# Rows of x and B through VectorE transposes and DRAM in a hybrid SSD / short-conv / gated decoder step

## The chip, the cores and the metric

The kernel runs on 1 core of one Trainium2 chip. The metric is the device time of one execution in microseconds. The profile is one more execution of the same program with the hardware profiler on. The engines are named as in the profile: PE is TensorE, DVE is VectorE, ACT is ScalarE, POOL is GpSimd, SP is SyncE, which issues most transfers.

## The reference, cut to what matters

One layer of a decoder step is computed in float32 for 336 tokens (16 meta tokens, 256 prompt tokens, 8 samples of 8 tokens) with D_MODEL 2048. The normalised tokens go through one input projection, whose columns feed two branches. Branch A is a state-space scan (SSD) over 64 heads of 64 columns, in 8 groups of 8 heads; each group shares one B and one C of 128 states. Branch B is a short gated convolution. Both are gated, merged and projected once more.

```python
xbc = silu(causal_dwconv(xbc, conv_prev, ssd_conv_w) + ssd_conv_b)
xs, bm, cm = split(xbc)                        # x: 64 heads x 64, B and C: 8 groups x 128
dt = softplus(dt_raw + dt_bias); log_a = dt * -exp(a_log); acum = cumsum(log_a)
wts = (cm . bm) * exp(acum_i - acum_j) * dt_j  # within a chunk, causal
y_diag = wts @ xs
chunk_states = sum_j exp(acum_last - acum_j) * dt_j * xs_j * bm_j
h = exp(acum_last) * h + chunk_states          # carried over the chunks; h0 for the samples
y = y_diag + (cm . h_in) * exp(acum) + d_skip * xs
y = group_rms_norm(y * silu(z)) * ssd_norm_w;  y_a = y @ w_ssd_out
x + (sigmoid(g_a) * y_a + sigmoid(g_b) * y_b) @ w_o
```

The outputs are the tokens after a final RMS norm and the new convolution and scan states.

## The kernel before, in words

**Layout.** Channels lie on partitions and tokens on the free axis, so a projection's 128 output channels come out as a tile of 128 x 320 to 336. A weight block is 128 x 1024 numbers (512 KB). `wblk` (L90) loads it on SP into `wraw`, ACT copies it into the rounded half `whi` (L94) and DVE makes the rest `wlo` (L96); each of the three has three buffers. `mm` (L108) multiplies it with the two halves of the tokens: `whi` by the high and the low half (L111, L112), `wlo` by the high half (L115), 24 matmuls for a block. A unit of a projection is two blocks that gather in one PSUM tile `pj` (two buffers). PSUM further has `ms` (two buffers) and `yb` (four banks).

**Stages.** First come the norm, branch B and the gates that need no scan, with the decay tables in between. Then the scan stage goes over the 8 groups g. In it these units run, each with its matmuls: four `z_units(g)` (the gate z, L496), eight `out_units(g-1)` (the projection of the group before, L733; one block each), six `conv_units(g+1)` (the convolution of the next group's B, C and four tiles of x, L481), and in the first and the last group four `gate_units`. The output projection ends the program.

**The scan as steps.** `ssd(g)` (L514) is a generator that does the scan of group g in steps, one at each `yield`. `weave` (L775) spreads a group's 23 steps over the units of the same group in proportion to their weights: z first, then out, gate, conv. `behind` (L99) binds the instructions of a step to come after the last weight block's on ACT, DVE and PE; within that the order on each engine is set by the planner of the framework, which also orders SP's transfers.

**What the change touches.** The scan needs x and B with tokens on partitions. `rows(c)` (L530), called for the three chunks of tokens (128, 128 and 80), makes them on PE: four transposes of x (L534) and one of B (L536) against the identity into two `ms` tiles, and beside them the product of B and C (L537). DVE scales x by dt from PSUM (L539), ACT and DVE split B in two halves (L546, L547) or copy it (L542), and DVE masks the product (L551). Further steps: `decay` (L554), `weights` (L564), `halve` (L572, splits the scaled x into the one buffer `xw`), `state` (L582, the chunk's state on PE), then `po` (L636, the samples' old states) and `yb` (L650, the scan's output). After that the samples' rows are put in order through the DRAM buffers `xq_d` and `bq_d` (L669 to L687), the norm of the group is made (L692 to L705), the samples' new states are made and stored (L713 to L719), and `yh`, `yl` (L722 to L728) are what `out_units` multiplies in the group that follows. The old states `h0` are loaded by four transfers of 512 KB in one step (L605 to L609).

## Time and profile before

| what | value |
|---|---|
| time, median of 3 runs (lowest to highest) | 1823.0 us (1822.77 to 1824.39) |
| time of the profiled execution | 1824.75 us |
| its span, first to last instruction | 1823.0 us |
| PE busy | 1814.9 us |
| DVE, ACT, POOL busy | 1147.7, 828.8, 389.4 us |
| granted PE clock | 1.0 |
| one group of the scan stage (902.00 to 1013.45 us) | 111.45 us, DVE 84.94, ACT 60.45, POOL 42.72 us busy |
| DMA in that group | 0.63 of the 16 engines, 201 GB/s |

A row of the groups' view reads: line, engine, operation, tiles out<-in, shapes, count, then the busy time, the mean of one in ns, and the idle time of the engine just before with what ended it. A row of the timeline reads: start, duration, engine, line, operation and tiles, count, and in brackets the idle time before it with what ended it. PE's matmuls overlap: each is shown from its issue to its end, so the cost of one on PE is the distance from its start to the next one's start.

### The profile page before, as it was taken

Reading aid. Unit: us, or ns where it says so; the run is one execution under the profiler, and the core shown is the slowest. Engines: PE = TensorE matmul, PEld = TensorE weight load, DVE = VectorE, ACT = ScalarE, POOL = GpSimd, SP = SyncE. Lnnn points to the kernel's source line nnn. Section 1 sums busy time; section 2 is a strip of 40 time slices with the busy share of each in tenths; the row PEclk is TensorE's granted clock in tenths of the full one; section 3 lists DMA queues with packets and bytes.
Section 4 is the critical chain, followed back from the end, with each engine's and each line's share of the span. In section 5 each row is a group of like instructions: output and inputs, shape, how many; then the busy total and the mean of one; then the engine's idle time right before and its main releaser. Section 6 shows DMA issues by size and latency. Waiting matters only on the chain.

```text
span 1823.0 us, 32410 instructions
## 1 busy us (share of the span) xinstructions
PE 1814.9 (100%) x13006; PEld 1798.0 (99%) x13006; DVE 1147.7 (63%) x1696; ACT 828.8 (45%) x1269; POOL 389.4 (21%) x398
## 2 busy tenths in 40 slices
PE   9999999999999999999999999999999999999998
PEld 9999999999999999999999999999999999999998
DVE  7745544444543335668587787877778777776544
ACT  6433333333333334645656354564546545343543
POOL 0000000000000001253162433524334252400012
PEclk9999999999999999999999999999999999999999
DMA  7444444444444446457566574665656657476553
GB/s 254 146 151 150 150 149 149 145 152 151 156 152 159 160 162 227 149 178 240 163 201 223 177 246 150 208 215 178 238 157 211 206 169 249 153 243 213 184 175 129
DMA packets 117286, 331.33 MB, mean 182 GB/s; under 512 B 20944, under 2 KB 37904, under 8 KB 117136
## 3 DMA queue, kind: packets, MB, share of 16 engines
q1 hardware_dynamic: 116272, 327.89, 55.9%
q8 instruction: 102, 1.67, 0.4%
q10 hardware_dynamic: 864, 1.38, 0.2%
q14 instruction: 48, 0.39, 0.1%
HBM read 296.34 MB, written 32.88 MB: 181 GB/s over the span
## 4 chain that ended last, share of the span: by engine, by line
PE 96%; DMA 2%; ACT 1%; DVE 1%; issue 0%; POOLq 0%; POOL 0%; SPq 0%; ACTq 0%; DVEq 0%
PE pj L111 30%; PE pj L112 30%; PE pj L115 29%; PE yb L650 2%; DMA wraw<-w 1%; PE ms L636 1%; PE pj L219 1%; PE yb L585 1%; PE pj L862 1%; ACT whi L94 0%; PE ms L534 0%; ACT W L559 0%; PE ms L219 0%; DMA ssms<-h 0%; PE yb L713 0%
## 5 line engine op out<-in xcount | busy, mean ns | idle before, releaser
L111 PE MATMUL pj<-hx,whi 128*128 128x320 f32 (+3 forms) x2880 | 864.4, 312 | 0.0
L112 PE MATMUL pj<-hx,whi 128*128 128x320 f32 (+3 forms) x2880 | 860.6, 311 | 0.0
L96 DVE TENSOR_TENSOR wlo<-wraw,whi 128x1024 fp32r<-128x1024 f32 x470 | 596.8, 1270 | 413.9 <-ACT whi L94 206.8
L94 ACT ACTIVATE whi<-wraw 128x1024 fp32r<-128x1024 f32 x470 | 496.7, 1057 | 768.0 <-PE pj L112 628.1
L111 PEld LDWEIGHTS pj<-hx,whi 128*128 128x128 f32 x2880 | 540.7, 188 | 4.6 <-ACT pad L462 1.7
L112 PEld LDWEIGHTS pj<-hx,whi 128*128 128x128 f32 x2880 | 541.5, 188 | 0.1
L115 PE MATMUL pj<-hx,wlo 128*128 128x320 f32 (+3 forms) x2880 | 485.4, 310 | 0.0
L115 PEld LDWEIGHTS pj<-hx,wlo 128*128 128x128 f32 x2880 | 440.6, 188 | 0.0
L111 PE MATMUL pj<-yh,whi 128*128 128x320 f32 x512 | 153.5, 311 | 1.2 <-ACT zs L503 0.9
L112 PE MATMUL pj<-yl,whi 128*128 128x320 f32 x512 | 152.3, 309 | 0.0
L596 POOL TENSOR_TENSOR h<-h,decS 128x512 f32<-128x512 f32 x64 | 76.4, 1227 | 147.5 <-PE ms L636 147.5
L111 PEld LDWEIGHTS pj<-yh,whi 128*128 128x128 f32 x512 | 96.2, 188 | 3.1 <-ACT zs L503 1.4
L112 PEld LDWEIGHTS pj<-yl,whi 128*128 128x128 f32 x512 | 96.3, 188 | 0.6
L115 PE MATMUL pj<-yh,wlo 128*128 128x320 f32 x512 | 95.8, 309 | 0.0
L242 POOL COPY SCS<-up 128x2 f32<-128x2 f32 x16 | 18.2, 1139 | 359.2 <-DVE up L236 329.0
L744 DVE TENSOR_TENSOR yan<-yan,pj 128x320 f32<-128x320 f32 x112 | 54.2, 485 | 62.9 <-PE pj L115 61.3
L471 DVE SCALAR_TENSOR_TENSOR cacc<-pad,V,cacc 128x360 f32<-128x360 f32 (+1 forms) x144 | 89.5, 621 | 2.0
L464 POOL COPY pad<-cs 128x24 f32<-128x24 f32 x48 | 56.2, 1172 | 126.6 <-DVE cacc L471 115.5
L115 PEld LDWEIGHTS pj<-yh,wlo 128*128 128x128 f32 x512 | 80.4, 188 | 0.0
L111 PE MATMUL pj<-vhi,whi 128*128 128x320 f32 x256 | 75.5, 308 | 0.0
L112 PE MATMUL pj<-vlo,whi 128*128 128x320 f32 x256 | 75.5, 308 | 0.0
L465 POOL COPY cs<-pad 128x3 f32<-128x3 f32 x48 | 45.0, 938 | 82.5 <-ACT pad L462 82.0
(286 smaller groups left out, 1721.7 us busy)
## 6 DMA issues: line engine op xcount, KB each, us to landing
wraw<-w SPq DMA_DIRECT2D x346, 512.0 KB, 3.9
wraw<-wso SPq DMA_DIRECT2D x64, 512.0 KB, 3.5
wraw<-wsc SPq DMA_DIRECT2D x32, 512.0 KB, 3.8
h<-h0T SPq DMA_DIRECT2D x32, 512.0 KB, 4.9
ssms<-h SPq DMA_DIRECT2D x32, 512.0 KB, 4.2
wraw<-wo SPq DMA_DIRECT2D x32, 512.0 KB, 3.9
xq_d<-xe SPq DMA_DIRECT2D x16, 320.0 KB, 3.4
W<-ac_d SPq DMA_DIRECT2D x8, 576.0 KB, 6.4
```

What stands on the lines that cost most here:

```text
L94: latest["act"] = nc.scalar.activation(hi[:, :n], raw[:, :n], AF.Copy).ins
L96: latest["dve"] = nc.vector.tensor_tensor(lo[:, :n], raw[:, :n], fb(hi[:, :n]), sub).ins
L111: nc.tensor.matmul(out, w, xh(k0 + k), start=first and k == 0, stop=False)
L112: nc.tensor.matmul(out, w, xl(k0 + k), start=False, stop=False)
L115: latest["pe"] = nc.tensor.matmul(out, w, xh(k0 + k), start=False, stop=last and k == nk - 1).ins
L219: nc.tensor.matmul(pu[i][:, :T - t0], w[:, o:o + P], x[:, k, t0:], start=k == 0 and j == 0, stop=k == 15 and j == 2)
L464: nc.gpsimd.tensor_copy(smp[:, :, 0:3], cs[:, 1:9, :])
L465: nc.gpsimd.tensor_copy(cs[:, 0, :], pad[:, 272:275])
L471: nc.vector.scalar_tensor_tensor(acc[:, i0:], pad[:, i0 + k:360 + k], col(V_CW, 4 * j + k), acc[:, i0:], mult, add)
L596: nc.gpsimd.tensor_tensor(split(h0[b]), split(h0[b]), bc(hv(decS[:, b, :], g), [P, 8, HP]), mult)
L650: nc.tensor.matmul(yb[q * HP:(q + 1) * HP, t, t0:t0 + n], x[:, h * HP:(h + 1) * HP], w[:, h, :], start=i == 0, stop=i == 3)
L744: nc.vector.tensor_tensor(ya[:, m, :TV], ya[:, m, :TV], pp[:, :TV], add)
```

## The change

Five things change together.

1. **Rows of x and B.** `rows(c)` and its PE transposes are gone. At the end of each convolution of B and of the four x tiles, DVE transposes the result in blocks of 32 x 32 (two instructions) into the convolution's buffer `acc` (tile `cacc`). Four transfers on ACT's queue write it to a DRAM buffer `xr_d` with tokens as rows; they are collected in `pend` and issued by `flush` inside the next unit. The scan loads the rows back by `load(c)` on SP, and `rows_in(c)` scales x on DVE and splits B on ACT and DVE. `cross()` makes all three products of B and C in one step.
2. **Steps.** The scan has 24 steps. `weave` gives each part of a group a fixed number: seven beside the z units, three beside the first two conv units, seven beside the out units (in the first group two gate units), seven beside the other four conv units. All groups' steps form one chain, and group 0's z units get none, so the last seven steps of a group run beside the z units of the next one. In the last group ten steps run beside the out units and fourteen beside six gate units; the first group now has two gate units instead of four.
3. **PSUM.** `pj` has three buffers and `ms` one. The state of chunk 2 and three of the table tiles move to `pj`.
4. **h0 and sample rows.** The four loads of `h0` are one per step (`carried`). The samples' transfers through `xq_d` and `bq_d` stand in later steps, each behind the current weight load on SP (`after`). The norm's three working tiles move from `zs` to one tile in `W`'s buffers, and the norm's scaling has a step of its own, before `yh` and `yl`.
5. **SP's order.** `load`, `carried` and the samples' transfers are bound to come after the last weight load traced before them.

```diff
+    xr_d = [dr.tile([XR, 640], F32, name=f"xr_d{i}") for i in range(2)]
...
-        nc.sync.dma_start(raw[:, :n], src)
+        latest["sp"] = nc.sync.dma_start(raw[:, :n], src).ins
...
+    def after(ins, a):
+        tc.add_manual_dep(ins, a.name, mybir.DependencyInfo(mybir.DependencyClass.NoSync,
+                                                            mybir.DependencyReason.DATA), reason="step")
...
+            for k in ("act", "dve", "pe"):
+                if k in latest and ins.engine == latest[k].engine:
+                    after(ins, latest[k])
...
+        pt = ps.tile([P, 512], F32, name="pj", bufs=3)
...
+        pend = []
+        def flush():
+            while pend:
+                nc.scalar.dma_start(*pend.pop(0))
...
+        def conv_tile(src, j, t0, out, cs, rows=None):
...
             nc.scalar.activation(acc[:, i0:], pad[:, i0:360], AF.Identity, bias=col(V_CB, j), scale=col(V_CW, 4 * j))
+            flush()
...
+            if rows is not None:
+                nc.vector.transpose(acc[:, :320], out[:, :320])
+                nc.vector.transpose(acc[:, 320:XR], out[:, T - 32:])
+                to, c = rows
+                for a in range(0, P, 32):
+                    pend.append((to.rearrange("(b q) c -> q b c", q=32)[:, :, c + a:c + a + 32],
+                                 acc[a:a + 32, :XR].rearrange("p (b f) -> p b f", f=32)))
...
-            conv_tile(w1[64 + g], 32 + g, 0, BT, cs[:, 4])
+            conv_tile(w1[64 + g], 32 + g, 0, BT, cs[:, 4], (to, 512))
...
-                conv_tile(w1[32 + 4 * g + t], 4 * g + t, 0, xs[:, t, :], cs[:, t])
+                conv_tile(w1[32 + 4 * g + t], 4 * g + t, 0, xs[:, t, :], cs[:, t], (to, P * t))
...
-            def rows(c):
-                (t0, n), m = CH[c], NT[c]
-                pp = ps.tile([P, 512], F32, name="ms")
-                for t in range(4):
-                    nc.tensor.transpose(pp[:n, t * P:t * P + P], xs[:, t, t0:t0 + n], ident)
...
+            bt = [pb.tile([P, 2, P], F32R, name="bh0", bufs=1), free[:, 1024:1280].rearrange("p (i n) -> p i n", n=P),
+                  pb.tile([P, P], F32, name="bt", bufs=1)]
+            def load(c):
                 xdt[c] = big("xdt", 3)
-                nc.vector.tensor_tensor(split(xdt[c][:n]), split(pp[:n]), bc(hv(dtt[:n, c, :], g), [n, 8, HP]), mult)
...
+                b = bt[c] if c == 2 else fb(bt[c][:, 1, :])
+                rows = xr_d[g % 2]
+                for o, r, n in ((0, P * c, P),) if c < 2 else ((0, 256, 64), (64, 336, 16)):
+                    for d, q in ((xdt[c], slice(0, 512)), (b, slice(512, 640))):
+                        after(nc.sync.dma_start(d[o:o + n], rows[r:r + n, q]).ins, latest["sp"])
+            def carried(u):
+                h = pb.tile([P, 2, 512], F32, name="h0", bufs=4)
+                after(nc.sync.dma_start(h, h0T[g, :, 2 * u:2 * u + 2, :]).ins, latest["sp"])
+                h0.extend((h[:, 0, :], h[:, 1, :]))
+                h0t.append(h)
+            def cross():
+                pq = ps.tile([P, 512], F32, name="ms", bufs=1)
+                qs = [pq[:n, o:o + m] for o, m, (_, n) in zip((0, NT[0], NT[0] + NT[1]), NT, CH)]
+                for c, (t0, n) in enumerate(CH):
+                    nc.tensor.matmul(qs[c], BT[:, t0:t0 + n], CT[:, TGT[c]:TGT[c] + NT[c]], start=True, stop=True)
+                for c, (_, n) in enumerate(CH):
+                    m = NT[c]
+                    cbm[c] = pb.tile([P, m], F32, name=f"cbm{c}", bufs=1)
+                    u0 = META if c == 0 else 0
+                    for a, b, to in ((0, m, 0),) if c < 2 else ((META, 80, 0), (0, META, 64)):
+                        nc.vector.tensor_tensor(cbm[c][:n, to:to + b - a], qs[c][:, a:b],
+                                                U[:, u0 + a:u0 + b] if c < 2 else UQ[:, a:b], mult)
+            def rows_in(c):
+                n = CH[c][1]
+                nc.vector.tensor_tensor(split(xdt[c][:n]), split(xdt[c][:n]), bc(hv(dtt[:n, c, :], g), [n, 8, HP]), mult)
+                if c < 2:
+                    b = fb(bt[c][:, 1, :])
+                    nc.scalar.activation(bt[c][:, 0, :], b, AF.Copy)
+                    nc.vector.tensor_tensor(bt[c][:, 1, :], b, fb(bt[c][:, 0, :]), sub)
...
-                pst = ps.tile([P, 512], F32, name="ms") if c == 2 else ps.tile([P, 4, 512], F32, name="yb", bufs=1)[:, 0]
+                pst = ps.tile([P, 512], F32, name="pj", bufs=3) if c == 2 else ps.tile([P, 4, 512], F32, name="yb", bufs=1)[:, 0]
...
             yield
-            rows(0)
+            cross()
+            load(0)
+            load(1)
             yield
             decay(0)
+            load(2)
             yield
             nc.scalar.activation(E, W[1], AF.Exp)
-            rows(1)
-            for u in range(4):
-                h = pb.tile([P, 2, 512], F32, name="h0", bufs=4)
-                nc.sync.dma_start(h, h0T[g, :, 2 * u:2 * u + 2, :])
-                h0 += [h[:, 0, :], h[:, 1, :]]
-                h0t.append(h)
-            yield
+            carried(0)
+            yield
+            decay(1)
+            carried(1)
+            yield
+            rows_in(0)
             weights(0)
+            carried(2)
             yield
             halve(0)
-            decay(1)
-            yield
-            rows(2)
+            carried(3)
+            rows_in(1)
             yield
             carry(0)
             state(0, pieces(0))
             weights(1)
             yield
             halve(1)
+            rows_in(2)
             decay(2)
             yield
             carry(1)
...
+            yield
+            shrink(6, 8)
+            for t in range(1, 4):
+                nc.gpsimd.tensor_tensor(zs[0][:, :TV], zs[0][:, :TV], zs[t][:, :TV], add)
+            yield
+            xq, bq = xq_d[g % 2], bq_d[g % 2]
+            for r in range(2):
+                for d, q in ((xq[:, 2 * r:2 * r + 2, :], xe2), (bq[:, r:r + 3:2, :], bhh)):
+                    after(nc.sync.dma_start(d, fb(q[:80])).ins, latest["sp"])
+            zq = pb.tile([P, 4, TV], F32R, name="zq", tag="yh", bufs=1)
+            nc.scalar.activation(zq[:, 0, :], zs[0][:, :TV], AF.Copy)
+            nc.vector.tensor_tensor(zq[:, 1, :], zs[0][:, :TV], fb(zq[:, 0, :]), sub)
+            yield
+            pr = ps.tile([P, 512], F32, name="ms", bufs=1)
+            for i in range(2):
+                nc.tensor.matmul(pr[:, :TV], onesR, zq[:, i, :], start=i == 0, stop=i == 1)
+            rms = pb.tile([P, 3, 384], F32, name="rms", tag="W")
+            x, rs, a = (rms[:, i, :TV] for i in range(3))
...
+            yield
+            for t in range(4):
+                y = ys[:, t, META:]
+                nc.vector.scalar_tensor_tensor(y, y, col(V_SNW, 4 * g + t), rs, mult, mult)
...
-                yield
                 if u == 0:
...
                     yield
+            yh = pb.tile([P, 4, TV], F32R, name="yh", bufs=1)
+            yl = pb.tile([P, 4, TV], F32R, name="yl", bufs=1)
+            for t in range(4):
+                y = ys[:, t, META:]
+                nc.scalar.activation(yh[:, t, :], y, AF.Copy)
+                nc.vector.tensor_tensor(yl[:, t, :], y, fb(yh[:, t, :]), sub)
...
                 nc.scalar.activation(z[:, :TV], pz, AF.Copy)
+                flush()
                 nc.vector.scalar_tensor_tensor(z[:, :TV], th, 1.0, z[:, :TV], add, mult)
...
-        def weave(parts, steps):
-            total, past, done = sum(n * w for _, n, w in parts), 0, 0
-            for w in (w for units, _, w in parts for _ in units):
-                past += w
-                want = NSTEP * past / total
...
-                while done + 1 <= want + 1e-6 and next(steps, "end") != "end":
-                    done += 1
-                behind(tail)
-            for _ in steps:
-                pass
+        def weave(parts):
+            for units, n, k in parts:
+                done = 0
+                for i, _ in enumerate(units):
+                    tail = nc.cur_bb.bb.instructions[-1]
+                    while done < k * (i + 1) // n:
+                        next(steps)
+                        done += 1
+                    behind(tail)
 
         S = [{} for _ in range(NG)]
         for _ in conv_units(0, S[0]):
             pass
+        steps = chain.from_iterable(ssd(g, S[g]) for g in range(NG))
         for g in range(NG):
...
+            last = g == NG - 1
+            parts = [(z_units(g, S[g]), 4, 7 if g else 0)]
+            if not last:
+                conv = conv_units(g + 1, S[g + 1])
+                parts.append((islice(conv, 2), 2, 3))
+            parts.append((out_units(g - 1, S[g - 1]), 8, 10 if last else 7) if g else (gate_units(0, 2), 2, 7))
+            parts.append((gate_units(2, 8), 6, 14) if last else (conv, 4, 7))
+            weave(parts)
```

More of the change, by code (lines that the diff above doesn't have):

```diff
@@ L1 @@
 from contextlib import ExitStack
+from itertools import chain, islice
 import concourse.bass as bass
@@ L102, in behind @@
                 break
-            for a in latest.values():
-                if ins.engine == a.engine:
-                    tc.add_manual_dep(ins, a.name, mybir.DependencyInfo(mybir.DependencyClass.NoSync,
-                                                                         mybir.DependencyReason.DATA), reason="step")
+            for k in ("act", "dve", "pe"):
+                if k in latest and ins.engine == latest[k].engine:
+                    after(ins, latest[k])
     def mm(out, hi, lo, xh, xl, base, nk, k0, first, last):
@@ L117, in unit @@
     def unit(src, xh, xl, n):
-        pt = ps.tile([P, 512], F32, name="pj")
+        pt = ps.tile([P, 512], F32, name="pj", bufs=3)
         for half in range(2):
@@ L129, in rstd @@
         spans = [(a, a + w) for a in (0, w, nt - w)]
-        pt_ = ps.tile([P, 512], F32, name="ms")
+        pt_ = ps.tile([P, 512], F32, name="ms", bufs=1)
         for c, (a, b) in enumerate(spans):
@@ L141, in rstd @@
         yield
-        pb_ = ps.tile([P, 512], F32, name="ms")
+        pb_ = ps.tile([P, 512], F32, name="ms", bufs=1)
         for i in range(2):
@@ L170, in tile_hybrid_step @@
     with tc.tile_pool(name="pa", bufs=2) as pa:
-        pu = [ps.tile([P, 512], F32, name=n) for n in ("pj", "pj", "ms")]
+        pu = [ps.tile([P, 512], F32, name="pj", bufs=3) for _ in range(3)]
         warm = pa.tile([P, 256], F32, name="warm", bufs=1)
@@ L185, in tile_hybrid_step @@
         nc.scalar.activation(prim, warm[:, 1:2], AF.Copy)
-        pw = ps.tile([P, 512], F32, name="ms")
+        pw = ps.tile([P, 512], F32, name="ms", bufs=1)
         for _ in range(WARM):
@@ L374, in tables @@
             yield
-            pp = ps.tile([P, 512], F32, name="ms")
+            pp = ps.tile([P, 512], F32, name="ms", bufs=1)
             for c, (t0, n) in enumerate(CH):
@@ L408, in tables @@
             yield
-            pc = ps.tile([P, 512], F32, name="ms")
+            pc = ps.tile([P, 512], F32, name="ms", bufs=1)
             for c, r in ((1, P), (2, META)):
@@ L415, in tables @@
             seg = CM[:80, C_SEG:C_SEG + NB].unsqueeze(2)
-            pc = ps.tile([P, 512], F32, name="ms")
+            pc = ps.tile([P, 512], F32, name="pj", bufs=3)
             for i, l in enumerate((lah, lal)):
@@ L520, in ssd @@
             ys = pb.tile([P, 4, T], F32, name="ys", bufs=1)
-            W, xdt, xe, bt, cbm, hst = ([None] * 3 for _ in range(6))
+            W, xdt, xe, cbm, hst = ([None] * 3 for _ in range(5))
             W[0], W[1] = (pb.tile([P, 8, PX], F32, name="W")[:, :, :n] for n in (P - META, PX))
@@ L631, in ssd @@
             yield
-            po = ps.tile([P, 512], F32, name="ms")
+            po = ps.tile([P, 512], F32, name="ms", bufs=1)
             for b in range(NB):
@@ L666, in ssd @@
             yield
-            xq, bq = xq_d[g % 2], bq_d[g % 2]
-            for r in range(2):
-                nc.sync.dma_start(xq[:, 2 * r:2 * r + 2, :], fb(xe2[:80]))
-                nc.sync.dma_start(bq[:, r:r + 3:2, :], fb(bhh[:80]))
             zs = st["zs"]
@@ L675, in ssd @@
             shrink(3, 6)
+            yield
[16 more added lines that the diff above has]
+            x, rs, a = (rms[:, i, :TV] for i in range(3))
+            nc.scalar.activation(rs, pr[:, :TV], AF.Abs_reciprocal_sqrt, scale=1.0 / 512, bias=eps4)
+            nc.vector.tensor_scalar(x, pr[:, :TV], 1.0 / 512, 4.0 * EPS, mult, add)
+            for _ in range(2):
+                nc.vector.scalar_tensor_tensor(a, rs, -0.5, x, mult, mult)
+                nc.vector.tensor_tensor(a, a, rs, mult)
+                nc.vector.scalar_tensor_tensor(rs, a, 1.5, rs, add, mult)
             yield
@@ L744, in out_units @@
                         nc.vector.tensor_tensor(ya[:, m, :TV], ya[:, m, :TV], pp[:, :TV], add)
+                flush()
                 yield
@@ L850, in tile_hybrid_step @@
             nc.sync.dma_start(xr, xk[:, m, META:META + NA])
-            po = ps.tile([P, 512], F32, name="pj")
+            po = ps.tile([P, 512], F32, name="pj", bufs=3)
             for half in range(2):
@@ L893, in tile_hybrid_step @@
         with tc.issue_after(first):
-            p1 = ps.tile([P, 512], F32, name="ms")
+            p1 = ps.tile([P, 512], F32, name="ms", bufs=1)
             for i in range(2):
```

79 lines of the change are left out of this document (15 added, 64 removed).

## The prediction

> **What bounds the kernel now.** I read the page first: busy times, the clock, then the chain that ended last.
>
> ```profile
> span 1823.0 us, 32410 instructions
> PE 1814.9 (100%) x13006; PEld 1798.0 (99%) x13006; DVE 1147.7 (63%) x1696; ACT 828.8 (45%) x1269; POOL 389.4 (21%) x398
> ...
> PEclk9999999999999999999999999999999999999999
> ...
> PE 96%; DMA 2%; ACT 1%; DVE 1%; issue 0%; POOLq 0%; POOL 0%; SPq 0%; ACTq 0%; DVEq 0%
> ```
>
> PE is busy for 1814.9 of 1823.0 us at the full clock, and 96% of the chain is PE. A busy PE need not be PE at its best, because matmuls overlap; so next come the waits of PE itself, and what its two suppliers of weights wait for.
>
> ```profile
> PE ms L188 <- DVE warm L173: 1.2, 1, 1.2
> PE pj L111 <- ACT zs L503: 0.9, 1, 0.9
> PE pj L827 <- POOL rs_r L823: 0.3, 1, 0.3
> PE pj L111 <- DVE yan L744: 0.3, 1, 0.3
> ...
> ACT whi L94 <- PE pj L112: 628.1, 313, 3.2
> ...
> ACT whi L94 <- DMA wraw<-w: 76.7, 28, 5.7
> ```
>
> PE waits 2.7 us in all. ACT, which makes `whi`, stood still before 313 blocks because PE had not yet given a buffer back, and before 28 because a load was late. So weights are mostly made ahead, and a microsecond taken off PE comes off the end, as long as the suppliers keep up. One group of the scan stage shows how full they are:
>
> ```profile
> 902.00:1013.45 111.45, 111.45 (x840) 109.69 (x839) 84.94 (x129) 60.45 (x106) 42.72 (x40) 1.00 0.63 201
> ```
>
> The columns after the window's 111.45 us are PE, PEld, DVE, ACT and POOL busy, the clock, the DMA share and GB/s. DVE has 26.5 us to spare, ACT 51, DMA 37% of its engines.
>
> **The change part by part.** *PE transposes removed.* The price of a matmul on PE is the distance to the next one's start, not its duration:
>
> ```profile
> 862.00 0.31 PE L111 MATMUL pj<-hx,whi 128*128 128x320 f32 x1
> 862.15 0.31 PE L112 MATMUL pj<-hx,whi 128*128 128x320 f32 x1
> 862.29 1.33 PE L115 MATMUL pj<-hx,wlo 128*128 128x320 f32 x8
> 863.46 0.60 PE L534 MATMUL ms<-CR,xs 128*128 128x128 f32 x4
> 863.90 0.27 PE L536 MATMUL ms<-CR,BT 128*128 128x128 f32 x1
> 864.01 0.37 PE L537 MATMUL ms<-CT,BT 128*128 128x112 f32 x2
> 864.15 0.39 PE L111 MATMUL pj<-hx,whi 128*128 128x320 f32 x1
> 864.38 0.31 PE L112 MATMUL pj<-hx,whi 128*128 128x320 f32 x1
> ```
>
> The five transposes of a chunk last from 863.46 to 864.01: 0.55 us, 0.11 each. Their number is in the groups:
>
> ```profile
> L534 PE MATMUL ms<-CR,xs 128*128 128x128 f32 (+1 forms) x96 | 14.4, 272 | 0.0
> ...
> L536 PE MATMUL ms<-CR,BT 128*128 128x128 f32 (+1 forms) x24 | 6.5, 272 | 0.0
> ```
>
> 96 + 24 = 120, times 0.11: **-13.2 us** (with both stamps rounded to 0.01, -13.0 to -13.4). The 80-token chunk has the same 128 moving columns.
>
> *Products of B and C in one step.* After L537 the first L111 takes 0.23 us to the next start, where 0.15 is usual (862.00 to 862.15): 0.08 for the product still running. Three such places per group become one: at most 2 x 8 x 0.08 = 1.3 us less, and 0 if the rest is then paid between the products. I take **-0.6**.
>
> *Third accumulator.* The waits on L503 and L744 above, 0.9 + 0.3 us, are PE waiting for a `pj` to be emptied. With a third one it waits a unit later: **-1.2**, at worst 0. `ms` goes to one buffer; its three uses in a group (products, `po`, norm) stand in steps 2, 13 and 18, with whole units between, so it costs 0.
>
> *DVE.* The only transpose in blocks in the trace, and the scaling that stays:
>
> ```profile
> L539 DVE TENSOR_TENSOR xdt<-ms,dtt 128x512 f32<-128x512 f32 (+1 forms) x24 | 16.4, 682 | 1.2 <-PE ms L534 1.2
> ...
> L643 DVE STREAM_TRANSPOSE xe<-xe 128x256 f32<-128x256 f32 x8 | 3.6, 446 | 0.3
> ```
>
> For 352 instead of 256 columns: 0.446 x 352 / 256 = 0.61 us a tile, five tiles, 3.1 us a group (4.5 if each of the two instructions took a whole 0.446). The scaling reads SBUF instead of PSUM; I keep 0.68. DVE goes to 88 of about 110 us: hidden, and 0 on the path. Gone from DVE's queue is the wait for PE's transposes.
>
> *ACT's queue.* Twenty transfers a group are issued by ACT, four at a flush. Nearest rows are SP's, for transfers cut into small or spread pieces:
>
> ```profile
> L406 SPq DMA_DIRECT2D ac_d<-acT x4: 486/594/1155, 538.2 to 540.6; - x4
> ...
> L670 SPq DMA_DIRECT2D bq_d<-bhh x16: 593/598/1338, 796.3 to 1568.9; - x16
> ```
>
> Minimum, median, maximum in ns. At 0.6 us: 12 us a group, ACT 72 of 110; at 1.34: 27 us, ACT 87. Behind a flush stand the next `whi` and the emptying of `pj`; four issues hold them for 2.4 us (5.4 at most). ACT's lead is up to three blocks of 24 matmuls, 3 x 24 x 0.15 = 10.5 us, so 0. The convolution's buffer is written again two units later (2 x 48 x 0.15 = 14 us) and must wait for its transfer to land. The nearest landings, from issue, are a write of 160 pieces and a read of 1024:
>
> ```profile
> W<-ac_d SPq DMA_DIRECT2D x8, 576.0 KB, 6.4
> ...
> bq_d<-bhh SPq DMA_DIRECT2D x16, 80.0 KB, 3.8
> ```
>
> With four behind each other some 4 to 8 us, so 0.
>
> *Transfers.* Written: 20 x 352 pieces of 128 B a group; read back: 672 pieces of 512 B or 2 KB. A stretch with mostly small pieces gives a price:
>
> ```profile
> DMA packets 867, 0.84 MB, mean 282 GB/s; under 512 B 617, under 2 KB 745, under 8 KB 867
> ...
> q1 hardware_dynamic: 867, 0.84, 94.5%
> ```
>
> In 3 us (697 to 700) 94.5% of 16 engines is 45.4 us for 867 packets: 52 ns each. By bytes alone a 128 B piece would be 7 ns. At 52, 7712 x 0.052 = 403 engine-us join the 0.63 x 111.45 x 16 = 1123 of a group: 0.87 of 16 x 109.7. Not the bound, so 0 on average. On SP the eight loads stand behind weight loads in the first conv units, four z units (4 x 48 x 0.15 = 29 us) after the last write was issued. SP has room:
>
> ```profile
> SPq L92 <- DVE wlo L96: 1070.3, 406, 9.1
> ...
> SPq L607 <- DMA ssms<-h: 37.2, 28, 3.5
> ```
>
> It stands mostly waiting for a free weight buffer. The second row is the load of `h0`, which waits for the store of the last group's states from the same buffers; with `carried` it comes at least three units after that store, so the wait goes. That it delayed weights shows in the chain:
>
> ```profile
> 1288.63 5.81 DMA wraw<-w
> ...
> 1301.79 6.68 DMA ssms<-h
> 1308.52 0.33 SPq L607
> 1308.95 8.10 DMA wraw<-w
> ```
>
> A store, the `h0` load behind it, then a weight load of 8.1 us, and PE only just did not stop. Gain from that: 0, as PE did not wait.
>
> *Moved steps.* Between `state(0)` and `state(1)`, which share the buffer `xw`, now stand two out blocks instead of three, 7 us of PE. What must happen in it:
>
> ```profile
> 887.76 0.60 ACT L589 ACTIVATE hst<-yb 128x512 f32<-128x512 f32 x1
> 888.25 0.62 ACT L573 ACTIVATE xw<-xe 128x512 fp32r<-128x512 f32 x1
> ...
> 888.44 1.25 POOL L579 TENSOR_TENSOR hst<-hst,cdec 128x512 f32<-128x512 f32 x1 [3.33 <-ACT hst L589]
> 889.65 1.29 POOL L574 TENSOR_TENSOR xw<-xe,xw 128x512 fp32r<-128x512 f32 x1
> ```
>
> From 887.76 to 890.94, 3.2 us: it fits, if nothing of 4 us stands ahead of it on ACT or POOL. In the first and last group steps stand closer. New seams of this kind will cost something; I take **+1.2**, as much as PE now loses on `pj`, between 0 and 1 us in each of 8 groups.
>
> *Sum:* -13.2 - 0.6 - 1.2 + 1.2 = -13.8. The profiled execution took 1824.75 us (1.75 more than its span), which becomes 1811.0. It was 1.75 above the median of the three runs, 1823.0; for the median I forecast **1809.2**. With every gain whole and no new wait it is -15.9: 1807.1.
>
> **The rivals.** *A, new seams cost 1 us in every group* (a flush ahead of a `whi`, `xw` late): 8 us, 1816. For: the z units have run out of lead before (28 late loads). Against: the covers above are two to three times what they hide.
>
> *B, the freed time turns into waits for weights.* If loads, ACT and DVE pace the z units, PE gets there sooner and waits: the 13.2 come back, 1822. For: the chain above, off PE from 1288.63 to 1317. Against: there it was the `h0` load, which the change moves, and PE waited only 1.2 us in the stage.
>
> *C, small writes fill the DMA engines* (slower). Place: the conv units and all behind them. It decides from (1755 - 1123) / 7712 = 82 ns a piece, 1.6 times the row above. At 93 ns a group lasts (1123 + 717) / 16 = 115.0 us, 3.6 more than now, in the seven groups with conv units +25: 1848; at twice the row, 104 ns, 120.3 us a group and 1885. Against: pieces in that row are larger, and by bytes it would be 7. The Trainium skill (DMA: Bandwidth & Descriptors, Specifications) says that below 512 B an engine reads, modifies and writes; that would be the doubling. No run here shows a 128 B write.
>
> *D, DVE takes PE's place* (slower). If all 8 x 3.1 us of its transposes came onto the path: 1834. It decides from (109.7 - 84.9) / 5 = 5 us a tile, eight times the 0.61 worked out above; that and its 26 us to spare speak against it. The Trainium skill (VectorE: DVE Perf Modes, Rules for kernel authors) would side with D: it keeps a full 128 x 128 transpose on TensorE where PSUM will do as its target. The rows decide by which engine is full.
>
> That the change does nothing is no case: the 120 instructions are gone from a full PE.
>
> **How the numbers follow.** Forecast 0.68, A 0.14, B 0.07, C 0.09, D 0.02. A measurement of this kernel tells 0.2%, 3.6 us, from no change. The forecast and A are faster (0.82), B is the same (0.07), C and D are slower (0.11). The likeliest's own range is 1807 to 1814; down to 1806.5 for the scatter of the median, and up to 1821, through A and part of B, it leaves out C, D and the rest of B.
>
> **What would show it.** Right: no L534 or L536 rows, their PE starts closed up; a group of 109 to 110 us; PE's waits still under 4 us; DVE about 88, ACT 70 to 75 us busy and issuing a group; h0 loads that wait for no store. Wrong: PE waiting at L111 for ACT or DVE in conv units (A); many `whi` waiting for `wraw` in z units (B); a DMA share near 1 in conv units and weights landing in over 8 us (C).

## The result, and the profile after

| | before | after |
|---|---|---|
| median of 4 runs (lowest to highest) | 1823.7 us (1822.77 to 1824.47) | 1893.76 us (1890.9 to 1896.35) |
| ratio, 95% interval | | 1.0384 [1.0366, 1.0402] |
| span of the profiled execution | 1823.0 us | 1889.1 us |
| PE's waits in it | 2.7 us | 58.6 us |
| mean granted PE clock | 1.000 | 0.988 |

The kernel became 3.8% slower, where 0.8% faster was forecast. Two executions of e7 below took 2945.85 and 4552.61 us, far from its other five, and its ratio leaves them out. The page of the changed kernel:

```profile
span 1889.1 us, 32435 instructions
PE 1825.1 (97%) x12886; PEld 1801.7 (95%) x12886; DVE 1203.0 (64%) x1776; ACT 826.9 (44%) x1261; POOL 328.8 (17%) x398
...
PE 13%; DVE 1%; DMA 1%; ACT 1%; issue 1%; POOL 0%; SPq 0%; POOLq 0%; ACTq 0%; DVEq 0%
```

PE has 120 instructions fewer and yet no shorter busy time, and the chain that ended last can't be followed through most of the span (the shares add up to 17%). So the waits of PE are read first, then one group, from PE's resumption in a conv unit to the same place a group later.

```profile
PE pj L116 <- ACT whi L96: 46.3, 23, 4.5
PE yb L620 <- POOL xw L609: 5.3, 2, 4.0
PE pj L116 <- DVE yan L787: 3.0, 4, 0.8
PE ms L193 <- DVE warm L178: 1.2, 1, 1.2
PE pj L120 <- DVE wlo L98: 1.2, 1, 1.2
```

```profile
1077.87:1198.10 120.23, 112.16 (x824) 109.52 (x824) 94.11 (x145) 58.71 (x100) 33.52 (x41) 0.99 0.64 201
```

The new wait is for `whi` (L96), the half of the weights that ACT makes: 46.3 us in 23 places, three in every group of the middle. (Rows left out add 1.6 us; `ya`, the sum that the out units add up, is the tile `yan` in the views.) A group takes 120.2 us, where 111.45 was the old and 109.7 the forecast time; DMA stands at 0.64 of its engines as before, and DVE still has 26 us to spare.

**The first of the three places** is in the conv units; PE waits 0.95 us there each time, 6.7 us in all. The timeline of ACT, with DVE's last transpose and PE's resumption:

```profile
1066.55 0.62 ACT L698 ACTIVATE xe<-xe 80x512 fp32r<-80x512 f32 x1
1071.28 1.86 ACTq L466 DMA_DIRECT2D xr_d<-cacc  x4
1074.80 1.68 ACT L708 ACTIVATE zs<-ys 128x320 f32<-128x320 f32 x4 [7.63 <-DVE ys L707]
1076.38 0.38 ACT L473 ACTIVATE pad<-pj 128x272 f32<-128x272 f32 x1
1076.65 0.22 ACT L474 ACTIVATE pad<-pj 128x64 f32<-128x64 f32 x1
1076.76 1.05 ACT L96 ACTIVATE whi<-wraw 128x1024 fp32r<-128x1024 f32 x1
...
1071.08 0.16 DVE L494 STREAM_TRANSPOSE cacc<-xs 128x32 f32<-128x32 f32 x1
...
1077.87 0.42 PE L116 MATMUL pj<-hx,whi 128*128 128x336 f32 x1 [0.95 <-ACT whi L96]
```

ACT is free at 1067.17. The next thing in its queue is the write of an x tile (L466), and DVE makes the last transpose of that tile only at 1071.08 to 1071.24. ACT stands still for 4.1 us with a transfer at the head of its queue, then issues for 1.9 us, then waits for DVE again in the squares (L708); `whi` follows 9.6 us after ACT came free. The planner had put the squares ahead of this `whi` too, and they had their input only at 1074.80, so the write alone doesn't explain the delay. Over all 160 issues, ACT stood still 63.6 us before 30 of them with DVE's transpose as the last to finish, and 12.9 us before 8 with the landing of another transfer.

**The second** is in the z units, and the dearest, 21.5 us in all:

```profile
1091.63 0.31 ACTq L466 DMA_DIRECT2D xr_d<-cacc  x1
1091.69 0.43 ACT L523 ACTIVATE zs<-pj 128x320 f32<-128x320 f32 x1
1094.44 1.36 ACTq L466 DMA_DIRECT2D xr_d<-cacc  x3
1095.83 1.28 ACT L728 ACT_TABLE_LOAD   x1 [3.71 <-issue]
1097.12 0.53 ACT L728 ACTIVATE rms<-ms,eps 128x320 f32<-128x320 f32 x1
1097.67 1.28 ACT L522 ACT_TABLE_LOAD   x1
...
1099.61 2.01 ACT L96 ACTIVATE whi<-wraw 128x1024 fp32r<-128x1024 f32 x2
...
1100.72 0.63 PE L116 MATMUL pj<-hx,whi 128*128 128x320 f32 x1 [4.54 <-ACT whi L96]
```

Here one write goes out and the other three stand from 1091.94 to 1094.44; a weight load landed at 1094.42. A completion semaphore tells that a transfer has landed. In this program the transfers of SP and ACT take turns on eight of them (the trace has 993 transfers, 124 or 125 on each), and each waits until the one before it on its semaphore has landed: none of the 993 was issued earlier. The second write and that weight load had the same semaphore. So a late write also holds up SP:

```profile
SPq L94 <- DMA xr_d<-cacc: 43.9, 8, 8.9
```

Eight weight loads, which have nothing to do with `xr_d`, waited 43.9 us for writes to it, up to 8.9 us each. Six of the eight, and 43.2 us, have one and the same form: the load was next on the semaphore of the first of B's four writes.

**The third** is the first out block, 15.2 us in all. SP's timeline, then ACT's, then PE's resumption:

```profile
1121.28 0.50 SPq L560 DMA_DIRECT2D xdt<-xr_d  x1
...
1126.55 0.42 SPq L560 DMA_DIRECT2D bt<-xr_d  x1
1127.06 0.84 SPq L94 DMA_DIRECT2D wraw<-wso  x2
...
1132.51 0.39 ACT L473 ACTIVATE pad<-pj 128x260 f32<-128x260 f32 x1 [3.28 <-PE pj L120]
...
1133.68 1.99 ACT L96 ACTIVATE whi<-wraw 128x1024 fp32r<-128x1024 f32 x2
...
1134.77 0.42 PE L116 MATMUL pj<-yh,whi 128*128 128x320 f32 x1 [1.75 <-ACT whi L96]
```

Eight row loads take 5.7 us of issuing, and the weights of the out units stand behind them. But the first of these weights landed at 1130.56, 3.1 us before `whi` began. What held `whi` then was ACT's queue: ahead of it stands `pad` (L473), which waits for PE's own last matmul of the unit. So at this place PE waits for an op that stands behind one that waits for PE. Whether the planner chose that order because of the burst is not shown.

**The clock.** The stretches before and after two of the stalls, with the granted clock as the third number from the right (the columns are those of the prediction's window):

```profile
1097.00:1100.40 3.40, 0.00 (x0) 0.00 (x0) 2.61 (x6) 3.36 (x6) 0.00 (x0) 1.00 0.45 155
1100.40:1103.80 3.40, 3.08 (x11) 3.08 (x12) 3.37 (x6) 2.16 (x3) 0.00 (x0) 0.50 0.09 25
1103.80:1107.20 3.40, 3.40 (x25) 3.40 (x25) 3.04 (x6) 0.86 (x1) 0.00 (x0) 1.00 0.89 268
...
1011.60:1015.00 3.40, 1.65 (x14) 1.50 (x13) 2.65 (x7) 3.21 (x6) 0.33 (x2) 1.00 0.95 327
1015.00:1018.40 3.40, 3.40 (x15) 3.40 (x15) 3.40 (x5) 3.40 (x7) 2.45 (x2) 0.51 0.67 173
```

After the stall of 4.54 us PE ran 3.4 us at half clock: 11 matmuls where the next stretch has 25. After one of 1.75 us (ended at 1013.97) it did too. The clock's record has ten such stretches before the last matmul, eight of 3.41 us and two of 6.83, 41.0 us together, so 20.5 us of work lost. (The mean of 0.988 also holds a stretch behind the last matmul, where nothing is lost.)

**Where the time went.** 1823.0 + 55.9 (waits) + 20.5 (clock) = 1899.4; the span is 1889.1, so PE's own work fell by 10.3 us. Of the work, three quarters of what was forecast went; what the forecast had taken as covered showed itself as waits.

### The profile page after: what moved, and what is told of

The parts are those of the page before. It is cut to its first block, busy times and chain, and to the rows that moved or that the text cites. A ratio compares the mean times of both kernels' runs of the same rounds, so it can differ in the third digit from the quotient of the medians.

```text
span 1889.1 us, 32435 instructions
## 1 busy us (share of the span) xinstructions
PE 1825.1 (97%) x12886; PEld 1801.7 (95%) x12886; DVE 1203.0 (64%) x1776; ACT 826.9 (44%) x1261; POOL 328.8 (17%) x398
## 3 DMA queue, kind: packets, MB, share of 16 engines
q10 hardware_dynamic: 59744, 8.60, 2.7%
## 5 line engine op out<-in xcount | busy, mean ns | idle before, releaser
L96 ACT ACTIVATE whi<-wraw 128x1024 fp32r<-128x1024 f32 x470 | 494.1, 1057 | 692.3 <-PE pj L117 540.8
L476 POOL COPY cs<-pad 128x3 f32<-128x3 f32 x48 | 31.4, 654 | 271.6 <-ACT pad L473 172.4
L486 ACT ACTIVATE cth<-cacc 128x360 f32<-128x360 f32 (+1 forms) x48 | 23.9, 499 | 75.7 <-DVE cacc L483 75.7
```

What stands on the lines that cost most here:

```text
L96: latest["act"] = nc.scalar.activation(hi[:, :n], raw[:, :n], AF.Copy).ins
L476: nc.gpsimd.tensor_copy(cs[:, 0, :], pad[:, 272:275])
L486: nc.scalar.activation(th[:, i0:], acc[:, i0:], AF.Tanh)
```

## The experiments

Two theories at first. *Q*: the writes on ACT's in-order queue hold `whi` back. *S*: the new placing of the steps does. All times are medians, the kernel before run beside each (1822.8 to 1823.7).

### Which half of the change: e1, e2

e1 keeps the steps and makes the rows on PE again:

```diff
             def rows_in(c):
+                t0, n = CH[c]
+                pp = ps.tile([P, 512], F32, name="ms", bufs=1)
+                for t in range(4):
+                    nc.tensor.transpose(pp[:n, t * P:t * P + P], xs[:, t, t0:t0 + n], ident)
...
-            load(0)
-            load(1)
```

> The changed kernel with one part undone: the rows of x and B come from 120 PE transposes again, so the DVE transposes, the 160 small writes on ACT's queue and the loads of the rows are gone. The new placing of the steps, the spread loads of h0 and the three accumulators stay. Theory Q (the writes on ACT's in-order queue hold whi back and PE starves; the clock drops after the stalls add to it): the stalls go with the writes, PE does the 13 us of transposes again, so about 1823 us, 1810 to 1830, waits of PE on whi under 15 us. Theory S (the new placing of the steps causes the stalls: seven steps beside z, more work of ACT and SP's bursts in few units): stays at 1870 us or above, with PE waits on whi of 30 us or more.

Measured: **1829.04 us**, 1.0030 [1.0018, 1.0042]. PE's waits:

```profile
PE pj L116 <- DVE yan L783: 4.3, 1, 4.3
PE ms L193 <- DVE warm L178: 1.2, 1, 1.2
PE yb L619 <- ACT xw L607: 1.0, 1, 1.0
PE yb L619 <- POOL xw L608: 0.5, 1, 0.5
```

Not one wait recurs in the groups; 4.3 us is in the last group and 1.5 in the first. S falls for the groups and holds for the two ends, at 5.5 us.

e2 is the converse: the steps and `weave` of before, the new rows.

```diff
+            load(0)
+            load(1)
             yield
             rows(0)
+            load(2)
```

> The kernel before with only the rows changed: DVE transposes, the 160 writes on ACT's queue, loads of the rows on SP; the placing of the 23 steps, the loads of h0 in one step and two accumulators of each kind are those of before. Theory Q: slow as the change, 1860 to 1910 us, with PE waiting on whi behind the writes. Theory S: 1805 to 1825 us. If both are needed together (ACT is full only where the writes meet the new steps): between, 1825 to 1855.

Measured: **1865.07 us**, 1.0231 [1.0215, 1.0246]. The rows alone cost 41.5 us, with the new steps 64.7 (1893.76 - 1829.04). The stalls are not quite the same ones, though, since the loads here stand close behind the last write:

```profile
SPq L557 <- DMA xr_d<-cacc: 87.9, 18, 8.9
```

SP's row loads themselves wait 87.9 us for the writes, with weights behind them. So e2 says that the new rows are the costly half, not by which queue.

### What of the writes costs: e3, e5, e6, e4

e3 has no writes, e5 has them from a constant tile, so that none waits for DVE, and e6 has the wait without the writes:

```diff
-                for a in range(0, P, 32):
+                for a in ():
```

```diff
                     pend.append((to.rearrange("(b q) c -> q b c", q=32)[:, :, c + a:c + a + 32],
-                                 acc[a:a + 32, :XR].rearrange("p (b f) -> p b f", f=32)))
+                                 CM[a:a + 32, :XR].rearrange("p (b f) -> p b f", f=32)))
```

```diff
-                nc.scalar.dma_start(*pend.pop(0))
+                nc.scalar.activation(*pend.pop(0))
...
+                pend.append((sink, acc[:, XR - 1:XR], AF.Copy))
```

> The changed kernel without the 160 writes: the transposes on DVE and the loads stay, the loads read zeros that are put in DRAM once at the start; the rows of x and B are therefore left out of the scan's states. Theory Q: 1805 to 1820 us, the waits on whi gone (under 10 us). Theory S, or SP's burst of row loads as the cause: the waits ahead of the out blocks stay, about 1850 us or more.

> The changed kernel, but the 160 writes read a constant tile in place of the transposed rows, so that no write waits for DVE; the DVE transposes are still done, the number, size and place of the writes are the same. The rows of x and B are left out of the scan's states (constants stand for them). With the writes 1893.8 us and without them 1837.7, the 56 us between divide into the issuing itself and the waiting of ACT's queue for DVE's transposes. If the issuing (9 us of ACT a group, and completion semaphores shared with SP's loads) is what costs: 1880 to 1895. If the waiting for the transposes is: 1838 to 1850. Both in part: between.

> The changed kernel without the writes, but at each of the 40 places where four writes stood ACT copies one column of the transposed tile, so that it waits for DVE's transposes as the writes did. The rows of x and B are left out of the scan's states (the loads read zeros). If ACT's waiting for the transposes is what costs: 1870 to 1895. If the issuing of the writes is: 1838 to 1850.

Measured: e3 **1837.66**, e5 **1832.28**, e6 **1856.06 us** (ratios 1.0070 [1.0053, 1.0087], 1.0049 [1.0034, 1.0064], 1.0178 [1.0163, 1.0193]). The waits for `whi` in e3, then in e5:

```profile
PE pj L116 <- ACT whi L96: 2.7, 2, 1.9
```

```profile
PE pj L116 <- ACT whi L96: 4.5, 4, 1.9
```

160 writes cost nothing if they need not wait: e5 is even 5 us below e3. So the issuing, 73 us of ACT in the changed kernel and 64 in e5, was rightly priced at 0. They do not stand at their places, though, which e5 was expected to keep: the planner, free of the wait, spread a group's twenty singly or in twos and threes over 44 us beside the out units' `whi`. Waiting for the transposes without any write costs 18.4 us (e6 - e3); the writes that wait cost 56.1 (1893.76 - 1837.66), three times as much.

The 18.4 us compare like with like, as ACT's order is the same in e3 and e6, and PE lost them for `ya` (16.8 against 8.3 us) more than for `whi` (5.1 against 2.7). The 56.1 us do not. In e3, e5 and e6 one `whi` stands ahead of the squares at the first place and two ahead of `pad` at the third; in the changed kernel all stand behind. So it is shown that waiting costs, and that the writes of the changed kernel cost more than the wait alone; how much of that is the landing of transfers and how much the order that the planner then chose is not.

The expectations of e3, e5 and e6 all missed. 1837.66 (e3) lies between 1820 and 1850, so something else costs too; 1856.06 (e6) lies between the two that were named, and 1832.28 (e5) below both.

e4 issues the writes on POOL:

```diff
-                nc.scalar.dma_start(*pend.pop(0))
+                nc.gpsimd.dma_start(*pend.pop(0))
```

> The changed kernel with the 160 writes issued by POOL, which is busy 18% of the span, in place of ACT. Theory Q: ACT is free of them, 1805 to 1825 us. If the price of such an issue on POOL holds up POOL's own work (xw, E, the copies of cs) for the scan: PE waits on POOL, 1825 to 1880. Theory S: 1860 or more.

Measured: **1864.07 us**, 1.0221 [1.0205, 1.0236]. PE's longest waits in e4, then an op of DVE in its groups' view:

```profile
PE pj L116 <- DVE yan L787: 17.5, 15, 2.2
PE pj L116 <- ACT whi L96: 5.7, 6, 1.9
```

```profile
L707 DVE TENSOR_TENSOR ys<-ys,zs 128x320 f32<-128x320 f32 x32 | 33.6, 1108 | 0.3
```

And the same op in e3:

```profile
L711 DVE TENSOR_TENSOR ys<-ys,zs 128x320 f32<-128x320 f32 x32 | 19.8, 677 | 0.3
```

ACT is free, and PE waits for `ya` on DVE instead. The DVE op took 1108 ns on average, in place of 677 in e3 and 513 in the changed kernel. That POOL's issuing does this was not tested by itself.

### SP's burst: e7, e8

```diff
             cross()
             load(0)
-            load(1)
             yield
             decay(0)
-            load(2)
             yield
             nc.scalar.activation(E, W[1], AF.Exp)
-            carried(0)
+            load(1)
             yield
             decay(1)
-            carried(1)
+            load(2)
```

The four `carried` follow with `rows_in(0)`, `halve(0)`, `weights(1)` and `decay(2)`. e7 is that on e3, e8 on e4.

> The run without writes (1837.7 us) with one further change: the eight loads of rows of a group, which stand with the loads of W in the steps of one conv unit, are put one chunk a step over three later steps, and the loads of h0 two to three steps later. The rows are left out of the scan's states as there. If SP's burst of loads ahead of the next weights is what keeps that run above 1810 to 1820: 1815 to 1828. If DVE's late additions to ya in the out units are (8.3 us of PE's waits there), or the waits on xw in the first and last group: no change, 1835 to 1840.

> The run with the writes issued by POOL (1864.1 us) with the loads of the rows and of h0 spread as in the run before this; nothing is left out. If SP's burst is what costs there (the first weights of the out units came 2.9 us late to ACT behind it): 1835 to 1855, and ACT's waits for wraw in the out units go. If POOL's issuing is what costs: 1860 to 1870.

Measured: e7 **1827.39** (10.3 below e3), e8 **1851.62 us** (12.5 below e4), ratios 1.0018 [1.0003, 1.0033] and 1.0158 [1.0143, 1.0173]. In e7 no wait for `whi` is left. The burst, with the loads of `h0` that were moved along, is a second cause, and adds to the first.

### The repairs, one on top of the other: e9, e10, e11

e9 binds each write behind the op that fills the next unit's buffer; e10 adds the spread; e11 sets the steps of the first and last group apart.

```diff
-            nc.scalar.activation(acc[:, i0:], pad[:, i0:360], AF.Identity, bias=col(V_CB, j), scale=col(V_CW, 4 * j))
-            flush()
+            flush(nc.scalar.activation(acc[:, i0:], pad[:, i0:360], AF.Identity, bias=col(V_CB, j),
+                                       scale=col(V_CW, 4 * j)).ins)
...
-                nc.scalar.dma_start(*pend.pop(0))
+                after(nc.scalar.dma_start(*pend.pop(0)).ins, a)
```

```diff
-            parts = [(z_units(g, S[g]), 4, 7 if g else 0)]
+            parts = [(z_units(g, S[g]), 4, 7 if g else 3)]
...
-            parts.append((out_units(g - 1, S[g - 1]), 8, 10 if last else 7) if g else (gate_units(0, 2), 2, 7))
-            parts.append((gate_units(2, 8), 6, 14) if last else (conv, 4, 7))
+            parts.append((out_units(g - 1, S[g - 1]), 8, 8 if last else 7) if g else (gate_units(0, 2), 2, 4))
+            parts.append((gate_units(2, 8), 6, 16) if last else (conv, 4, 7))
```

> The changed kernel with one order added: each group of four writes stands on ACT behind the op that fills the next unit's conv buffer (in a z unit behind the copy of z), where the changed kernel's planner put them up to two ops earlier. Nothing is left out. The writes then ask for the transposes about 1 us later. Theory Q (ACT waits in its queue for DVE's transposes, and what is behind, whi above all, is late): most of the gap to the run with constant writes (1832.3 us) closes, 1835 to 1860. If what costs is that the writes are late themselves (SP's loads share their semaphores and wait up to 8.9 us for them): no better, 1880 to 1900.

> The run before this one with the loads of rows and of h0 spread over later steps, as in the two spread runs (there minus 10.3 and minus 12.5 us). If the two causes add: 10 to 13 us below the run before this. If the spread loads wait for later writes: no gain.

> The run before this one with the steps of the first and the last group set apart: first group 3 steps beside z (before 0) and 4 beside the two gate units (before 7), last group 8 beside its out units (before 10) and 16 beside the gate units (before 14). PE waited there for xw 5 to 6.5 us in all in every run with the new rows, and the clock was at half for 6.8 us and 3.4 us behind. If these waits come from halves and their products standing in neighbouring steps of short units: 8 to 11 us below the run before this; if moved only: within 2 us of it.

Measured: e9 **1855.17**, e10 **1842.73**, e11 **1831.68 us** (ratios 1.0174 [1.0157, 1.0192], 1.0101 [1.0086, 1.0116], 1.0041 [1.0026, 1.0056]): steps of -38.6, -12.4 and -11.1 us, each as its cause would have it. In e9 the semaphore coupling went with the late writes:

```profile
SPq L94 <- DMA xr_d<-cacc: 3.7, 5, 1.5
```

3.7 us in place of 43.9. ACT's wait for transposes ahead of a write fell from 63.6 to 0.6 us. The one edge moved more than the writes: one `whi` again stands ahead of the squares at the first place, and two ahead of `pad` at the third. So the 38.6 us are what the edge is worth together with the order that followed from it. One group of e11 by stretches, then PE's longest waits in it over the whole span:

```profile
1183.26:1295.08 111.82, 110.36 (x824) 108.10 (x824) 92.76 (x146) 58.37 (x100) 36.57 (x40) 1.00 0.67 212
```

```profile
PE pj L116 <- ACT whi L96: 10.9, 7, 2.4
PE pj L116 <- DVE yan L786: 4.3, 7, 1.1
```

### What is left: e12 to e16

e12 puts e11's setting apart (the second diff above) on e1. e13 is e11 with the last x tile's writes one z unit later and 6 and 18 steps in the last group; e14 is e12 with 6 and 18. e15 and e16 are e13 and e14 with 8 and 16 again, but none in the first out unit.

```diff
-                flush(nc.scalar.activation(z[:, :TV], pz, AF.Copy).ins)
+                zc = nc.scalar.activation(z[:, :TV], pz, AF.Copy).ins
+                if t:
+                    flush(zc)
```

```diff
+            if last:
+                out = out_units(g - 1, S[g - 1])
+                parts += [(islice(out, 1), 1, 0), (out, 7, 8)]
```

> The run with the rows by PE and the new steps (1829.0 us) with the same setting apart of the steps in the first and last group. PE waited 1.5 us for xw in the first group and 4.3 us for ya in the last, and the clock was at half for 6.8 us: 1819 to 1823 if both waits go with it, 1827 to 1831 if they only move.

> The run with ordered writes, spread loads and steps set apart (1831.7 us; PE waited 10.9 us for whi, in each group 1.1 to 2.4 us in the second z unit, where ACT had four writes, a table load and the norm ahead of three whi) with two further moves: the four writes of the last x tile stand one z unit later, and the last group has 6 steps beside its out units and 18 beside the gate units. If the writes ahead of the table load hold that whi: PE's waits for whi go to under 3 us and the time to 1815 to 1822, below the kernel before. If the norm's table load alone holds it: 1828 to 1832. The sum of the prediction (minus 13.8 us) with all covers intact would be 1809.

> The run with the rows by PE and the steps set apart (1826.4 us; its one wait of 3.7 us, in the last group, behind ACT's E that waited 6.6 us for the load of W) with 6 steps beside the last group's out units in place of 8. If that wait goes and with it the half clock behind it: 1820 to 1823, as the kernel before or 0.2% below. If it only moves: 1825 to 1828.

> The run with the writes of the last x tile one z unit later (1837.8 us), with the last group's steps as two runs before it (8 beside its out units, 16 beside the gate units) but none in the first out unit. That run's waits beside the groups' own were 4.0 us for zq and 2.2 us for ya with the half clock behind them. If they go: 1826 to 1830, between the kernel before and the run with steps set apart (1831.7). PE's own work was 110.7 us a group there against 111.4 before, so 1816 to 1818 is the floor of this arrangement with no wait at all.

> The rows by PE, the new steps, and the same arrangement of the last group: with 8 steps beside the out units PE waited 3.7 us for ya behind E's wait for the load of W, with 6 steps 4.0 us for zq. With the steps starting one out unit later, E's wait shrinks by 3.5 us: 1820 to 1824, no different from the kernel before, if both waits go; 1826 or more if a wait of another kind comes.

| | us | ratio, 95% interval | PE's waits left |
|---|---|---|---|
| e12 | 1826.39 | 1.0011 [1.0001, 1.0021] | `ya` 3.7, last group |
| e13 | 1837.79 | 1.0080 [1.0067, 1.0093] | `zq` 4.0, `ya` 6.9, `wlo` 3.2, `whi` 0.5 |
| e14 | 1829.49 | 1.0032 [1.0020, 1.0043] | `zq` 4.0, last group |
| e15 | 1832.60 | 1.0050 [1.0036, 1.0064] | `ya` 9.0, `wlo` 3.5, `whi` 1.0 |
| e16 | 1824.07 | 1.0007 [0.9998, 1.0016] | `xw` 0.7, last group |

e12, e13 and e14 came out at none of the times that were named for them. In e13 the wait for `whi` in the z units went (10.9 to 0.5 us, and 1.0 in e15), so the writes ahead of the table load did hold it; but the time rose by 6.1 us. Of that the `zq` wait and its half clock explain 4.0 + 1.7, as its twin in e14 has them:

```profile
PE ms L721 <- ACT zq L716: 4.0, 1, 4.0
```

e15, without that wait, came back only to e11's time, not to the 1826 to 1830 expected: a wait taken out of the z units returned as waits on `ya` and `wlo` in the out units. e16 removes all but 0.7 us of the waits that the new steps had brought and is not different from the kernel before. So the steps, the spread loads of `h0` and the third accumulator bring no gain that could be measured by themselves, and no version here beats the kernel before.

## Why the prediction was wrong, point by point

**PE transposes, -13.2, and products, -0.6: right in kind, a quarter too large.** Span less waits less clock loss is 1823.0 - 2.7 = 1820.3 before, 1889.1 - 58.6 - 20.5 = 1810.0 after, and 1828.0 - 18.3 = 1809.7 in e11, which has no stretch at half clock before the last matmul. PE's own work fell by 10.3 to 10.6 us. By the distances between starts the 96 transposes of x took 10.4 us, as forecast; without the 24 of B and with the products in one step 1.4 us went in place of 3.2, and the matmuls of the weights took 1 us more. It was a fall of work, not of time.

**ACT's queue, "so 0": the step that failed.** It weighed the time of issuing against a lead of 10.5 us. The time of issuing was right (median 476 ns against 600) and costs nothing (e5). What was not asked is what the transfer at the head of the queue waits for: DVE's transposes, in a unit in which DVE is busy with the step's other work, and the landing of an earlier transfer on its semaphore. Together they used up the lead: without the writes (e3) 56.1 of the 70 us went, and e9, whose one edge makes a write ask later, took back 38.6. How these divide between ACT's own wait (e6: 18.4), SP's loads behind the late writes, the planner's new order and the clock was not separated further. (The lead itself, 3 x 24 x 0.15, is 10.8.)

**SP's eight loads, "SP has room": failed.** On average it has. But the loads stand in one burst of 5.7 us ahead of the out units' weights: spreading them and the loads of `h0` took off 10.3 to 12.5 us in three pairs (e3 and e7, e4 and e8, e9 and e10).

**Moved steps, +1.2: mis-sized.** Seams in the groups cost nothing (e1), but the first and last group, of which the prediction said only that steps stand closer there, cost 5.5 us with the rows on PE and 11.1 with the new rows (e10 to e11).

**The clock: no term at all.** It added 20.5 us. The Trainium skill (TensorE: Matmul & The Clock Gate, Why this matters for your kernels) warns of idle gaps above some 3 us between matmuls. The trace agrees for 4.54 us, and shows more: the stall of 1.75 us that ended at 1013.97 was followed by half clock, and an equally long one that ended at 1134.77 was not. In these traces the place in time decides. All ten stretches at half clock begin on one grid of 3.413 us (the two shown begin at 1015.05 and 1100.38, 25 steps apart). The two intervals of that grid in which the two stalls lie, then the time behind the second:

```profile
1011.63:1015.04 3.41, 1.66 (x13) 1.51 (x13) 2.69 (x7) 3.25 (x6) 0.33 (x2) 1.00 0.96 330
1131.10:1134.51 3.41, 1.93 (x15) 1.77 (x14) 1.36 (x6) 1.92 (x4) 0.33 (x2) 1.00 0.95 286
...
1134.80:1138.20 3.40, 3.40 (x23) 3.40 (x24) 3.40 (x6) 3.40 (x5) 1.45 (x2) 1.00 0.71 207
```

The first stall lies whole within one interval, in which PE was idle for 1.75 us; the second is cut into 1.49 and 0.26. In the eighteen traces, from 140 us to the last matmul, each of the 50 intervals at full clock in which PE was idle for 1.86 us or more was followed by half clock. Of the five with 1.75 to 1.82 us two were, and none with less. This is read off the traces; no experiment was made for it.

**Third accumulator, -1.2: no gain.** PE's waits on the emptying of `pj` went from 1.2 us to 3.0 (after) and 4.3 (e11), because `ya`'s additions stand late on DVE. With the rows on PE again (e16) they are gone, and the time is that of before all the same.

**DVE, h0: right for the bound.** The transposes of a tile take 505 + 169 ns (0.61 forecast), 3.4 us a group, and DVE did not become the bound. In the group shown it is busy for 94.1 us, though, and not for 88: other ops grew longer beside them, which the sum had not asked about. No load of `h0` waits for a store any more.

```profile
L493 DVE STREAM_TRANSPOSE cacc<-xs x32: 497/505/516, 721.5 to 1569.9; 128x320 f32<-128x320 f32 x32
L494 DVE STREAM_TRANSPOSE cacc<-xs x32: 161/169/173, 722.0 to 1570.3; 128x32 f32<-128x32 f32 x32
```

**Rivals.** A had the place and the sign, "a flush ahead of a `whi`, `xw` late", but at 1 us a group; it was 58.6 - 2.7 = 55.9 us, 7 a group, before the clock. B's place came, late `whi` in the z units, but not its sign: ACT's `whi` waited for a load of `w` 31 times (55.6 us), before 28 times (76.7). C had the right side for the wrong reason, and D did not happen. C's price:

```profile
q10 hardware_dynamic: 59744, 8.60, 2.7%
...
xr_d<-cacc ACTq DMA_DIRECT2D x160, 44.0 KB, 3.7
```

0.027 x 16 x 1889.1 us / 59744 = 13.7 ns a piece: a quarter of the 52 used, and twice the 7 by bytes. The reading and modifying below 512 B that the Trainium skill states (DMA: Bandwidth & Descriptors, Specifications) would fit that, and so would a fixed part per piece; no run tells them apart.

## What to carry to other kernels

A transfer issued by a compute engine is an instruction that waits: before moving one onto a queue that also makes another engine's input, ask when its source is ready and what stands behind it, not how long issuing takes. Ask also what the planner puts behind what, as one edge changes more of the order than it names. Here one ordering edge, so that the transfers ask later, was worth 38.6 us, and the spreading of the loads 12. When the bound engine gives up work, forecast the waits that its slack has been covering, with the clock's loss after each; -10.3 us of work became +70 us of time.

## What the hardware showed that was not expected

- PE stalls of as little as 1.75 us can be followed by 3.4 us at half clock, which makes such a stall cost about twice its length. An equal one had no such stretch behind it: in these traces it goes by PE's idle time within one interval of a fixed grid of 3.413 us, with the border between 1.75 and 1.86 us.
- Transfers of SP and ACT that have no data in common were coupled by their shared completion semaphores: weight loads waited up to 8.9 us for small writes, and 43.9 us in all, until the writes were issued on time (3.7 us). The Trainium skill (DMA: Bandwidth & Descriptors, Issuing engines are not separate DMA queues) says that issuing from several engines saves only the issue time; no run here issues the same writes from SP to compare. What the trace shows beside it is that a transfer that waits stops the engine that issues it, 4.1 us at the first place.
- With POOL issuing the small writes, an unchanged DVE op on 128 x 320 took 1108 ns on average in place of 677 (e3) or 513 (the changed kernel); the cause was not tested by itself.
